# An opening in smaller loads, and breaks in the matmul order of the first three blocks (hybrid encoder layer, one core)

## The chip, the cores and the metric

The kernel runs on one core of a Trainium2 chip. Its time is the device time of one execution in microseconds; of several runs the median is given. Matrix products run on TensorE (PE in the profile, PEld for its weight loads), elementwise work on VectorE (DVE), ScalarE (ACT) and GpSimd (POOL). Transfers are issued by SyncE (SP) and by ScalarE.

## The reference

One encoder layer on 256 tokens of 2048 channels, in float32:

```python
hn = _rmsnorm(h, norm_w[i])
proj = hn @ w_in[i]                       # 2048 x 18432, nine groups of 2048 columns
q, v, f_fwd, f_bwd, z_a, b_gate, c_gate, h_b, z_b = jnp.split(proj, IN_SPLITS, axis=-1)
o_a = _hgrn2_bidirectional(jax.nn.silu(q), v, f_fwd, f_bwd, lb_all[:, i])
o_a = _head_rmsnorm(o_a, hgrn_norm_w[i]) * jax.nn.silu(z_a)
y_b = b_gate * _short_conv(c_gate * h_b, conv_w[i])
o_b = _rmsnorm(y_b, conv_norm_w[i]) * jax.nn.silu(z_b)
h = h + jnp.concatenate([o_a, o_b], axis=-1) @ w_out[i]
h = h + (p[i] @ w_ple[i]) * jax.nn.sigmoid(h @ w_ple_gate[i])
return _rmsnorm(h, final_norm_w)
```

The weights are large (211 MB are read) and the products with them are nearly all of the work.

## The kernel before

**Products in split form.** Every float32 operand is split into a high part, rounded to the matmul's format (fp32r), and the rest, a low part. ScalarE casts the high part (line 74), VectorE subtracts it (line 75). A product is then high times both parts plus low times high. In the blocks of this change (lines 299 to 312) a block is 256 output columns, over 16 k-tiles of 128 rows. For each k-tile and each half of 128 columns (m = 0, 1) there are two matmuls: a *long* one, the high part of the weights with both parts of x (512 columns, line 309), and a *short* one, the low part of the weights with the high part of x (256 columns, line 307). Four matmuls, each with its own weight load, make a tile of a block. Their order is `PLAIN`: long, short, long, short. A table can give single tiles another order: `OUTER` is long, short, short, long, and `SHORTS` is short, short, long, long. `ONE` and `BOTH` put such a break into tile 1, or into tiles 1 and 5, of some later blocks.

**Opening.** x comes transposed, scaled by the norm weights (`x_split`, lines 249 and 250: the high part on ScalarE, the low part on VectorE); the row norms come later, as a factor. The vectors (norm weights and nine others, 80 KB) are one load on ScalarE's queue (line 155). SP loads x and the weights: first k-tiles 0 and 1 of x, then of the first block's weights, then k-tiles 2 and 3 of both, then the rest in pieces of four k-tiles. Loads use eight semaphores in turn, so that a load waits on its queue until the load eight before it has landed. Meanwhile 13 matmuls of zeros run on TensorE (line 179).

**The first three blocks** (forward and backward forget gates and q of the first head pair) are worked through side by side: four groups g of four k-tiles, and in each the three blocks c = 0, 1, 2. This part is written in order by hand for ScalarE, VectorE and TensorE. With c = 0 comes the split of x. I call a pair (g, c) a part.

**Behind it** a planner orders the instructions of each engine by priorities and its own costs; TensorE works through block after block, and the recurrent mixing of the pair of heads (scans, exponentials, products on GpSimd, then small score matmuls, lines 506 and 550) is put in between at fixed numbers of tiles. The four matmuls `rps` (line 284), which spread the row norms, come behind the 14th tile of the fourth block.

Of the kernel before, what the change touches and what calls it, by code (L numbers as in the profile page):

```python
# [88 lines left out]
def tile_hymba_encoder(  # L89
# [14 lines left out]
    nc = tc.nc  # L104
# [16 lines left out]
    ws = Stream(tc, rawp, splp, 3)  # L121
# [29 lines left out]
    def load_x(k0, k1):  # L151
        nc.sync.dma_start(xf32[:, k0:k1], xt[:, k0:k1])

    vec = const.tile([P, 10, 16], F32, name="vec")
    nc.scalar.dma_start(vec, vecs)

    for k0 in (0, 2):
        load_x(k0, k0 + 2)
        ws.load(0, k0, k0 + 2)
    for g in range(4):  # L160
        if g:
            load_x(4 * g, 4 * g + 4)
# [12 lines left out]

    act.activation(dummy[:, 0:1], wz[:, 0:1], AF.Copy)
    wps = psm.tile([P, 512], F32, tag="y", name="wps")
    for _ in range(13):
        pe.matmul(wps[:, :P], lhsT=wz, rhs=wz, start=True, stop=True)

    epst = const.tile([P, 1], F32, name="epst")
# [35 lines left out]
    def lower_bounds():  # L217
        dve.tensor_tensor(out=mx, in0=th[:, :, 0, :], in1=th[:, :, 1, :], op=ALU.max)
        for j in range(2):
            dve.tensor_tensor(out=et[:, :, j, :], in0=th[:, :, j, :], in1=mx, op=ALU.subtract)  # L220
        act.activation(et, et, AF.Exp)
        dve.tensor_tensor(out=esum, in0=et[:, :, 0, :], in1=et[:, :, 1, :], op=ALU.add)
        dve.reciprocal(out=esum, in_=esum)
        dve.tensor_tensor(out=lb, in0=et[:, :, 0, :], in1=esum, op=ALU.mult)
        dve.tensor_scalar(lb, lb, 2.0**-63, None, op0=ALU.max)
        dve.tensor_tensor(out=oml, in0=et[:, :, 1, :], in1=esum, op=ALU.mult)
        dve.tensor_scalar(noml, oml, -1.0, None, op0=ALU.mult)
# [8 lines left out]
    def tick():  # L236
        now[0] += 1
        due = sorted(e for e in pend if e[0] <= now[0])
        for e in due:
            pend.remove(e)  # L240
        for e in due:
            e[2]()
# [5 lines left out]
    def x_split(kt):  # L248
        act.activation(xs[:, kt, 0, :], xf32[:, kt, :], AF.Copy, scale=nw[:, kt : kt + 1])
        dve.scalar_tensor_tensor(  # L250
            out=xs[:, kt, 1, :], in0=xf32[:, kt, :], scalar=nw[:, kt : kt + 1],
            in1=xs[:, kt, 0, :], op0=ALU.mult, op1=ALU.subtract,
        )
# [35 lines left out]
    def acc_in(c, i):  # L289
        return [psg.tile([P, 2, T], F32, tag="g", name=f"a{c}_{i}_{m}") for m in range(2)]  # L290
# [3 lines left out]
    OUTER = ((0, 0), (0, 1), (1, 1), (1, 0))  # L294
    SHORTS = ((0, 1), (1, 1), (0, 0), (1, 0))
# [3 lines left out]
    def gemm_part(acc, w, g, k0=0, k1=4, orders={}):  # L299

        for k in range(k0, k1):
            kt = 4 * g + k
            for m, short in orders.get(kt, PLAIN):
                a = acc[m].rearrange("p a b -> p (a b)")
                lhsT = w[:, k, short, m * P : (m + 1) * P]
                if short:
                    pe.matmul(a[:, :T], lhsT=lhsT, rhs=xs[:, kt, 0, :], start=False, stop=(kt == NKT - 1))  # L307
                else:
                    pe.matmul(  # L309
                        a, lhsT=lhsT, rhs=xs[:, kt, :, :].rearrange("p s n -> p (s n)"), start=(kt == 0), stop=False  # L310
                    )
            tick()
# [37 lines left out]
    ids3 = [blocks[c, 0] for c in first]  # L350
    acc3 = [acc_in(c, 0) for c in first[:2]]
    acc3.append([psm.tile([P, 2, T], F32, tag=t, name=f"a{B_Q}_0_{m}") for m, t in enumerate(("x", "y"))])
    with tc.manual_schedule(engines={ENG.Activation, ENG.DVE, ENG.PE}):
        for g in range(4):
            for c in range(3):
                half, v = ws.open(ids3[c][g])

                n = 2 if g or c else 1
                for k0 in range(0, 4, n):
                    if c == 0:  # L360
                        for k in range(k0, k0 + n):
                            x_split(4 * g + k)
                    ws.split(half[:, k0 : k0 + n], v[:, k0 : k0 + n])
                    gemm_part(acc3[c], v, g, k0, k0 + n)
            if g == 2:
                lower_bounds()
    rctx.close()
# [544 lines left out]
```

## Time and profile before

| | us |
|---|---|
| three timed runs | 1127.13, 1127.22, 1128.06 |
| median | 1127.22 |
| profiled execution | 1127.79 |
| its span in the trace | 1126.1 |
| TensorE busy in the span | 1116.5 |
| mean granted clock of TensorE | 0.998 |

The span begins with the first instruction and ends with the last; 1.69 us of the profiled execution lie outside it. A row of the timeline gives start and duration in microseconds, engine, line, operation, output and inputs; merged rows give their count, and in brackets stands how long the engine had been idle and for whom it waited. A matmul's duration includes its way through the array, so that successive matmuls overlap in the records; the pace is read from starts.

### The profile page before, as it was taken

What the parts mean: (1) busy time and instruction counts of PE and PEld (TensorE: products, weight loads), DVE (VectorE), ACT (ScalarE), POOL (GpSimd) and SP (SyncE); (2) the same over time, 40 slices, a digit from 0 to 9 for tenths busy, and PEclk for the clock granted to TensorE, in tenths of its full rate; (3) what the DMA queues carried; (4) which work ended last, traced back from release to release, by engine and by line L of the source; (5) the groups of instructions that cost most, each with busy time, mean ns of one, the idle gap of its engine ahead of it and who ended that gap; (6) DMA issues with size and microseconds to landing.
All of it is one profiled execution on the core that took longest, in us unless ns stands there. A gap on an engine that the chain in (4) does not pass through costs nothing.

```text
span 1126.1 us, 16341 instructions
## 1 busy us (share of the span) xinstructions
PE 1116.5 (99%) x6530; PEld 959.9 (85%) x6530; DVE 728.5 (65%) x920; ACT 629.4 (56%) x868; POOL 217.8 (19%) x167
## 2 busy tenths in 40 slices
PE   9999999999999999999999999999999999999996
PEld 8888888888888888888888888888888888888886
DVE  7798476956876587766655665565565555545664
ACT  7696577756775586564454454444445434444553
POOL 1144025300622034221121111121220000000112
PEclk9999999999999999999999999999999999999999
DMA  9746445555545455555555565555557555556542
GB/s 352 268 168 209 155 160 188 159 188 181 201 135 209 163 169 169 192 182 187 188 191 187 182 200 196 194 192 192 188 188 270 187 186 187 187 203 212 201 169 75
DMA packets 37371, 214.25 MB, mean 190 GB/s; under 512 B 4144, under 2 KB 4528, under 8 KB 17584
## 3 DMA queue, kind: packets, MB, share of 16 engines
q1 hardware_dynamic: 37008, 212.88, 54.4%
q8 instruction: 51, 0.84, 0.3%
q10 hardware_dynamic: 288, 0.34, 0.1%
q14 instruction: 24, 0.20, 0.1%
HBM read 211.11 MB, written 2.10 MB: 189 GB/s over the span
## 4 chain that ended last, share of the span: by engine, by line
PE 99%; ACT 0%; DVE 0%; DVEq 0%; issue 0%; ACTq 0%
PE a L309 37%; PE a L307 18%; PE a L330 5%; PE a L328 5%; PE a L329 5%; PE pg L736 3%; PE pg L735 3%; PE pg L737 3%; PE pa L735 3%; PE pa L736 3%; PE pa L737 3%; PE pb L736 3%; PE pb L735 3%; PE pb L737 3%; PE scps L506 1%; PE cx L550 1%
## 5 line engine op out<-in xcount | busy, mean ns | idle before, releaser
L75 DVE TENSOR_TENSOR spl<-raw,spl 128x1024 fp32r<-128x1024 f32 (+2 forms) x398 | 498.5, 1259 | 309.3 <-ACT spl L74 309.1
L309 PE MATMUL a<-xs,spl 128*128 128x512 f32 x1792 | 620.6, 394 | 0.0
L74 ACT CAST spl<-raw 128x1024 fp32r<-128x1024 f32 (+2 forms) x398 | 403.2, 1019 | 329.2 <-PE a L307 164.7
L307 PE MATMUL a<-xs,spl 128*128 128x256 f32 x1792 | 493.2, 278 | 0.0
L309 PEld LDWEIGHTS a<-xs,spl 128*128 128x128 f32 x1792 | 335.0, 188 | 76.9
L307 PEld LDWEIGHTS a<-xs,spl 128*128 128x128 f32 x1792 | 335.9, 188 | 1.9 <-DVE spl L75 0.2
L328 PE MATMUL a<-spl,xs 128*128 128x512 f32 x256 | 100.8, 394 | 0.0
L330 PE MATMUL a<-spl,xs 128*128 128x512 f32 x256 | 99.8, 390 | 0.0
L329 PE MATMUL a<-spl,xs 128*128 128x512 f32 x256 | 99.6, 389 | 0.0
L341 ACT COPY r<-a 128x256 f32<-128x256 f32 x112 | 40.9, 368 | 56.0 <-PE a L307 56.0
L795 POOL TENSOR_TENSOR hh<-hh,fw 128x512 f32<-128x512 f32 (+1 forms) x9 | 11.7, 1311 | 260.4 <-ACT gt L794 257.8
L330 PEld LDWEIGHTS a<-spl,xs 128*128 128x128 f32 x256 | 48.1, 188 | 10.1
L328 PEld LDWEIGHTS a<-spl,xs 128*128 128x128 f32 x256 | 48.1, 188 | 9.6
L329 PEld LDWEIGHTS a<-spl,xs 128*128 128x128 f32 x256 | 48.1, 188 | 9.5
L735 PE MATMUL pa<-spl,mixa 128*128 128x512 f32 x128 | 50.1, 392 | 0.0
L737 PE MATMUL pa<-spl,mixa 128*128 128x512 f32 x128 | 49.8, 389 | 0.0
L736 PE MATMUL pa<-spl,mixa 128*128 128x512 f32 x128 | 49.8, 389 | 0.0
L735 PE MATMUL pb<-spl,mixb 128*128 128x512 f32 x128 | 49.8, 389 | 0.0
L736 PE MATMUL pb<-spl,mixb 128*128 128x512 f32 x128 | 49.8, 389 | 0.0
L737 PE MATMUL pb<-spl,mixb 128*128 128x512 f32 x128 | 49.8, 389 | 0.0
L346 POOL TENSOR_TENSOR xf<-xf,rbc 128x1024 f32<-128x1024 f32 x8 | 19.8, 2477 | 131.1 <-DVE xf L342 124.0
L735 PE MATMUL pg<-spl,ht 128*128 128x512 f32 (+1 forms) x120 | 45.1, 376 | 0.0
(183 smaller groups left out, 1170.6 us busy)
## 6 DMA issues: line engine op xcount, KB each, us to landing
raw<-in_w_in_dram SPq DMA_DIRECT2D x106, 1024.0 KB, 4.9
raw<-in_w_in_dram SPq DMA_DIRECT2D x74, 512.0 KB, 4.9
raw<-in_w_out_dram SPq DMA_DIRECT2D x32, 1024.0 KB, 4.8
raw<-in_w_gate_dram SPq DMA_DIRECT2D x12, 1024.0 KB, 4.8
raw<-in_w_gate_end_dram SPq DMA_DIRECT2D x8, 512.0 KB, 4.8
xf<-in_xtok_dram SPq DMA_DIRECT2D x2, 1024.0 KB, 11.9
hh<-in_xtok_dram SPq DMA_DIRECT2D x1, 2048.0 KB, 8.0
raw<-in_w_ple_dram SPq DMA_DIRECT2D x4, 512.0 KB, 3.4
```

The source lines that it names most:

```text
L74: self.nc.scalar.copy(out=v[:, :, 0], in_=r)
L75: self.nc.vector.tensor_tensor(out=v[:, :, 1], in0=r, in1=v[:, :, 0], op=ALU.subtract)
L307: pe.matmul(a[:, :T], lhsT=lhsT, rhs=xs[:, kt, 0, :], start=False, stop=(kt == NKT - 1))
L309: pe.matmul(a, lhsT=lhsT, rhs=xs[:, kt, :, :].rearrange("p s n -> p (s n)"), start=(kt == 0), stop=False)
L328: pe.matmul(acc[m], lhsT=lh, rhs=w[:, kt % 2, 0, :], start=(kt == 0), stop=False)
L329: pe.matmul(acc[m], lhsT=lh, rhs=w[:, kt % 2, 1, :], start=False, stop=False)
L330: pe.matmul(acc[m], lhsT=ll, rhs=w[:, kt % 2, 0, :], start=False, stop=(kt == NKT - 1))
L341: act.copy(out=r, in_=acc[m][:, 1, :])
L346: pool.tensor_tensor(out=t, in0=t, in1=r.unsqueeze(1).broadcast_to([P, n, T]), op=ALU.mult)
L735: pe.matmul(acc[m], lhsT=lh, rhs=wh, start=(kt == 0), stop=False)
L736: pe.matmul(acc[m], lhsT=lh, rhs=wl, start=False, stop=False)
L737: pe.matmul(acc[m], lhsT=ll, rhs=wh, start=False, stop=(kt == nk - 1))
```

## The change

Four edits. The norm weights are loaded on their own (8 KB, 64 bytes a partition) ahead of the nine other vectors, both from ScalarE. The first two k-tiles of x and of the first block's weights come in pieces of one k-tile (128 KB each). The zero calls are 11 in place of 13. In six of the twelve parts of the first three blocks, from (0, 1) to (2, 0), the part's second tile gets a break, `OUTER` and `SHORTS` in turn.

```diff
     vec = const.tile([P, 10, 16], F32, name="vec")
-    nc.scalar.dma_start(vec, vecs)
-
-    for k0 in (0, 2):
-        load_x(k0, k0 + 2)
-        ws.load(0, k0, k0 + 2)
+    nc.scalar.dma_start(vec[:, 0], vecs[:, 0])
+    nc.scalar.dma_start(vec[:, 1:], vecs[:, 1:])
+
+    for k0, k1 in ((0, 1), (1, 2), (2, 4)):
+        load_x(k0, k1)
+        ws.load(0, k0, k1)
...
-    for _ in range(13):
+    for _ in range(11):
         pe.matmul(wps[:, :P], lhsT=wz, rhs=wz, start=True, stop=True)
...
+    turns = ((0, 1), (0, 2), (1, 0), (1, 1), (1, 2), (2, 0))
+    kicks = {(g, c): {4 * g + 1: (OUTER, SHORTS)[n % 2]} for n, (g, c) in enumerate(turns)}
...
-                    gemm_part(acc3[c], v, g, k0, k0 + n)
+                    gemm_part(acc3[c], v, g, k0, k0 + n, kicks.get((g, c), {}))
```

What it moves, from the order of instructions of both kernels. In the changed kernel's rows the line numbers are one higher up to the first three blocks, and four higher behind them. First TensorE in part (0, 1), tiles 0 and 1 (`a_0_0` and `a_0_1` are the block's two halves, `spl` the split weights). Before:

```order
L309 MATMUL a_0_0_167<-xs,spl_206 128x512
L307 MATMUL a_0_0_167<-xs,spl_206 128x256
L309 MATMUL a_0_1_168<-xs,spl_206 128x512
L307 MATMUL a_0_1_168<-xs,spl_206 128x256
L309 MATMUL a_0_0_167<-xs,spl_206 128x512
L307 MATMUL a_0_0_167<-xs,spl_206 128x256
L309 MATMUL a_0_1_168<-xs,spl_206 128x512
L307 MATMUL a_0_1_168<-xs,spl_206 128x256
```

and the same tiles of part (0, 2) in the changed kernel:

```order
L310 MATMUL a_0_0_170<-xs,spl_228 128x512
L308 MATMUL a_0_0_170<-xs,spl_228 128x256
L310 MATMUL a_0_1_171<-xs,spl_228 128x512
L308 MATMUL a_0_1_171<-xs,spl_228 128x256
L308 MATMUL a_0_0_170<-xs,spl_228 128x256
L308 MATMUL a_0_1_171<-xs,spl_228 128x256
L310 MATMUL a_0_0_170<-xs,spl_228 128x512
L310 MATMUL a_0_1_171<-xs,spl_228 128x512
```

The second tile has both shorts ahead of both longs; in part (0, 1) its order is long, short, short, long. Elsewhere TensorE's order is the same in both kernels but for the two zero calls.

SP at the start (`xf` is x, `raw` the weights as loaded; `DMAHW0` to `DMAHW7` are the eight semaphores, of which vec takes the first). Before:

```order
L152 DMA xf_80<-in_xt_dram 128x512
L58 DMA raw_84<-in_w_in_dram 128x512
L152 DMA xf_80<-in_xt_dram 128x512
L58 DMA raw_84<-in_w_in_dram 128x512
L58 DMA raw_88<-in_w_in_dram 128x512 x2
L58 DMA raw_91<-in_w_in_dram 128x1024
L152 DMA xf_80<-in_xt_dram 128x1024 [waits DMAHW0_49]
L58 DMA raw_84<-in_w_in_dram 128x1024 [waits DMAHW1_49]
```

Now:

```order
L152 DMA xf_80<-in_xt_dram 128x256
L58 DMA raw_85<-in_w_in_dram 128x256
L152 DMA xf_80<-in_xt_dram 128x256
L58 DMA raw_85<-in_w_in_dram 128x256
L152 DMA xf_80<-in_xt_dram 128x512
L58 DMA raw_85<-in_w_in_dram 128x512
L58 DMA raw_91<-in_w_in_dram 128x512 [waits DMAHW0_49]
L58 DMA raw_91<-in_w_in_dram 128x512 [waits DMAHW1_49]
L58 DMA raw_94<-in_w_in_dram 128x1024 [waits DMAHW2_49]
L152 DMA xf_80<-in_xt_dram 128x1024 [waits DMAHW3_49]
```

The waits begin with the second block's first half (`raw_91`); the third block's first load (`raw_94`) now waits for the second vec load.

ScalarE while the second head pair's forget gates are prepared (`lf` their logarithms, `dd` and `pf` the exponentials of the first pair, `sq` the gate of q). Before:

```order
L477 ACTIVATE dd_640<-dd_640 128x512
L399 ACT_TABLE_LOAD
L399 ACTIVATE lf_864<-xf_503,lb,oml 128x256 x2
L74 CAST spl_908<-raw_890 128x2x512
L399 ACTIVATE lf_864<-xf_503,lb,oml 128x256
L392 ACT_TABLE_LOAD
L392 ACTIVATE sq_861<-qt_504 128x512
```

Now:

```order
L480 ACTIVATE pf_640<-dd_641 128x512
L403 ACT_TABLE_LOAD
L403 ACTIVATE lf_865<-xf_504,lb,oml 128x256
L481 ACT_TABLE_LOAD
L481 ACTIVATE dd_641<-dd_641 128x512
L74 CAST spl_909<-raw_891 128x2x512
L403 ACT_TABLE_LOAD
L403 ACTIVATE lf_865<-xf_504,lb,oml 128x256 x2
L396 ACT_TABLE_LOAD
L396 ACTIVATE sq_862<-qt_505 128x512
```

One exponential of `pf` and the last of `dd` come later, between the logarithms, with two more table loads. VectorE's order changes in the same stretch in the same manner; GpSimd's order does not change.

## The prediction

> **What bounds the kernel now.** I read the page first (busy shares, then the chain of waits), then the opening 15 us row by row, then the pace of TensorE in stretches of equal work, and last the place near 110 us where the order on ScalarE changes.
>
> ```profile
> span 1126.1 us, 16341 instructions
> PE 1116.5 (99%) x6530; PEld 959.9 (85%) x6530; DVE 728.5 (65%) x920; ACT 629.4 (56%) x868; POOL 217.8 (19%) x167
> PE 99%; ACT 0%; DVE 0%; DVEq 0%; issue 0%; ACTq 0%
> ```
>
> TensorE is busy for 99% of the span and is 99% of the chain that ends last. The kernel can become faster only where TensorE starts its real work earlier, or where the same matmuls follow each other more closely. Both are small. The opening, from the timeline of the three engines:
>
> ```profile
> 1.12 5.37 PE L179 MATMUL wps<-wz 128*128 128x128 f32 x26 [1.12 <-DVE wz L174]
> 5.20 0.51 ACT L249 ACTIVATE xs<-xf,vec 128x256 fp32r<-128x256 f32 x1 [2.46 <-DMA vec<-in_vecs_dram]
> 5.81 0.41 ACT L74 CAST spl<-raw 128x256 fp32r<-128x256 f32 x1
> 6.37 0.47 PE L309 MATMUL a<-xs,spl 128*128 128x512 f32 x1
> 7.25 0.41 ACT L74 CAST spl<-raw 128x256 fp32r<-128x256 f32 x1
> 8.53 1.75 DVE L75 TENSOR_TENSOR spl<-raw,spl 128x256 fp32r<-128x256 f32 x3
> 9.08 0.31 PE L307 MATMUL a<-xs,spl 128*128 128x256 f32 x1
> 9.57 0.39 PE L309 MATMUL a<-xs,spl 128*128 128x512 f32 x1
> 11.40 1.29 DVE L75 TENSOR_TENSOR spl<-raw,spl 128x512 fp32r<-128x512 f32 x2 [1.13 <-ACT spl L74]
> 12.39 0.40 PE L309 MATMUL a<-xs,spl 128*128 128x512 f32 x1
> ```
>
> Zero matmuls fill TensorE from 1.12 us. ScalarE waits 2.46 us for the norm weights (5.20), casts the first weight tile (5.81), and the first real matmul starts at 6.37. The first four k-tiles are then paced by ScalarE and VectorE: the split of the fourth is the first of the three that start at 8.53, and its short matmul starts at 9.08, right behind it. The next part starts at 9.57.
>
> **Pace.** A k-tile is four matmuls: two long (512 columns, line 309) and two short (256 columns, line 307). I cut windows at the start of a tile, so that two hold the same 16 tiles, and a third holds the 57 tiles after the first four:
>
> ```profile
> 18.05:29.35 11.30, 11.30 (x34) 6.01 (x33) 1.00 1.03 415
> 148.74:159.83 11.09, 11.09 (x33) 6.00 (x33) 1.00 0.55 191
> 9.57:49.85 40.28, 40.28 (x115) 21.43 (x115) 1.00 0.85 339
> 50.55 0.60 PE L284 MATMUL rps<-ident,rw 128*128 128x128 f32 x4
> ```
>
> (The rows are those of line 309; the first number is the width, and the counts include matmuls that hang over an edge.) The same 16 tiles take 11.30 us early and 11.09 us later, at the same granted clock (1.00): 0.7067 us a tile (40.28/57 gives the same) against 0.6931 us, 13.6 ns less. TensorE waits for nothing in either window, so this is a state of the matmul stream, and it holds for 40 us: it ends where the four small matmuls of the norms (50.55) interrupt the stream.
>
> **The change part by part.**
>
> *Norm weights alone, smaller first pieces, fewer zero calls.* Three things must be there for the first real matmul: norm weights, a piece of x, a piece of weights.
>
> ```profile
> vec<-in_vecs_dram ACTq DMA_DIRECT2D x1, 80.0 KB, 4.4
> xf<-in_xt_dram SPq DMA_DIRECT2D x2, 256.0 KB, 4.4
> raw<-in_w_in_dram SPq DMA_DIRECT2D x4, 256.0 KB, 5.1
> q1 hardware_dynamic: 873, 1.65, 69.5%
> q10 hardware_dynamic: 144, 0.08, 5.6%
> 0.80 0.39 SPq L152 DMA_DIRECT2D xf<-in_xt_dram  x1
> 2.18 1.92 SPq L58 DMA_DIRECT2D raw<-in_w_in_dram  x4
> 5.19 0.33 SPq L152 DMA_DIRECT2D xf<-in_xt_dram  x1
> 2.00:4.00 2.00, 2.00 (x11) 2.00 (x11) 0.19 (x1) 0.73 (x2) 2.00 (x8) 1.00 0.91 223
> L179 PE MATMUL wps<-wz x26: 275/421/582, 1.1 to 6.2; 128*128 128x128 f32 x26
> ```
>
> Ahead of the first cast stood 80 + 256 + 256 = 592 KB (there at 5.81 at the latest); now 80 + 128 + 128 = 336 KB, what before had come by 5.20 (vec and the first x). So the first cast moves from 5.81 to about 5.2, and TensorE's first real matmul is ready near 5.2 + (6.37 - 5.81) = 5.8. The zero calls: 26 passes in 5.37 us, 22 of them end near 1.12 + 5.37 x 22/26 = 5.7. Removing two calls is thus needed for the earlier start, and by itself worth nothing. The start gains about 0.5 us.
>
> That gain does not last, I think. The third k-tile needs the second half of the first weight block. In the kernel before, ScalarE cast it at 7.25. After the change the same 80 + 1024 KB must still land ahead of that cast, in more packets. If it lands when it did, casts and splits of the third and fourth tiles run as before: fourth split from 8.53, next part at 9.57, and the gain is nil, since every short matmul there starts right behind its split. More packets: the 144 of vec took 5.6% of 16 engines over 8 us, 7.2 engine-us or 50 ns each; 144 more on 16 engines are at most 0.45 us, and at least nothing, since the bytes are equal. I take 0.1 us lost at 9.57, bounds 0.45 lost to 0.54 gained: the upper one because the third weight block's first half was split at 11.40 + 0.65 = 12.05, with its first matmul at 12.39 and its first short one a third of a tile, 0.24, later, so no earlier start can be worth more than some 0.34 + 0.24 = 0.58 less a semaphore, say 0.54, from there on unless that load comes earlier too.
>
> The issue order on SP hides one more thing. Eight loads are in flight on eight semaphores; the ninth waits for the first to land (5.19, when vec was there). Two vec loads and smaller pieces use them up sooner: the third block's 512 KB is now issued when the second vec load lands (about 5.2; before, it was the last of the four issued by 4.10). The cover is what is queued ahead of it: 80 + 4 x 128 + 4 x 256 KB, of which some 0.7 MB are there by 5.2 (at 223 GB/s, the stretch 2 to 4 us, from 2.0 on), so 0.9 MB are left, 2.2 us at 415 GB/s (the windows above). An issue reaches the engines in less: the first one starts at 0.80 and they are 0.91 busy from 2.00. Nothing is lost; without that cover the 1.2 us between issue and transfer would be.
>
> The Trainium skill, DMA: Bandwidth & Descriptors, section Issuing engines are not separate DMA queues, says that transfers issued from different engines share the same 16 engines and interleave. The trace agrees (80 KB on ScalarE's queue took 4.4 us, as 256 KB on SP's), and by it the rest of vec still gets in the way of the pieces behind it, which speaks for the lost 0.1 rather than the gain.
>
> *Breaks.* Six of the twelve parts of the first three blocks get one tile in another order: long-short-short-long (OUTER) in three, both shorts before both longs (SHORTS) in three. The number of matmuls and columns is the same. The kernel before has such breaks later; two of them, with the tile ahead and the tile behind:
>
> ```profile
> 52.38 0.39 PE L309 MATMUL a<-xs,spl 128*128 128x512 f32 x1
> 54.48 0.39 PE L309 MATMUL a<-xs,spl 128*128 128x512 f32 x1
> 126.51 0.39 PE L309 MATMUL a<-xs,spl 128*128 128x512 f32 x1
> 128.60 0.40 PE L309 MATMUL a<-xs,spl 128*128 128x512 f32 x1
> ```
>
> Three tiles with a SHORTS break take 2.10 and 2.09 us against 3 x 0.693 = 2.08: a break costs up to 0.02 us and leaves the quick pace quick. Whether one turns the slow pace into the quick one no row shows directly: at 126.51 it comes one tile after another kind of matmul, too soon to tell the pace ahead of it. What speaks for it: the pace changed at a single interruption (50.55) and never by itself in 57 tiles. I take it that the first SHORTS break does it. It sits in the tenth tile; the tiles behind it to the interruption are 61 - 10 = 51, worth 51 x 13.6 ns = 0.69 us, less 6 x 0.02 = 0.12 for the breaks: 0.57 us. Bounds: 0.12 lost to 0.76 gained (all 57 tiles quick at once, breaks free, is 0.78). No new wait: a broken tile is the second of a piece whose split the first has used already.
>
> *What the planner does with it.* Behind the first blocks the order on TensorE is unchanged, but on ScalarE two table loads are added between 78 and 90 us, and one exponential is moved behind an evacuation.
>
> ```profile
> 74.65 1.15 ACT L476 ACTIVATE pf<-dd 128x512 f32<-128x512 f32 x2
> 78.34 1.28 ACT L399 ACT_TABLE_LOAD   x1
> 86.88 1.98 ACT L74 CAST spl<-raw 128x1024 fp32r<-128x1024 f32 x2
> 87.95 2.36 DVE L75 TENSOR_TENSOR spl<-raw,spl 128x1024 fp32r<-128x1024 f32 x2 [0.21 <-ACT spl L74]
> 90.23 1.38 DVE L554 COPY_PREDICATED scm<-tri,scps 128x512 f32<-128x512 uint32 x2
> 105.51 0.62 POOL L487 TENSOR_TENSOR kc<-dd,ge 128x256 f32<-128x256 f32 x1
> 106.21 1.91 POOL L493 TENSOR_TENSOR kx<-kc,ge 128x512 f32<-128x512 f32 x1
> 110.25 1.27 PE scps L506 x63
> 111.52 1.09 PE cx L550 x8
> ```
>
> Two loads of 1.28 and one half of 1.15 are 3.1 us on ScalarE ahead of the two casts at 86.88. VectorE works in order: their subtractions (87.95) and the masked copies (90.23) move by as much, and behind those stand the scans from which GpSimd makes kc and kx for the second pair. kx ends at 108.12, so at 111.2; TensorE wants it at 111.52, less the 0.47 it is early by then, 111.05. The scores at 110.25 need only kc (106.13, then 109.2, against 109.8). So kx comes about 0.2 us late: I take 0.2 lost, bounds 0 and 1.3 (one table load more than I count, 1.28).
>
> **Sum.** -0.57 (pace) + 0.1 (start) + 0.2 (kx) = -0.27 us. The profiled execution took 1127.79 us, its span and 1.69 around it: it becomes 1127.5. The three timed runs have a median of 1127.22, 0.57 below the profiled one, so the timed median becomes 1126.95; I say **1126.9 us**.
>
> **Rivals.**
> 1. *Breaks change nothing in the pace.* For it: the same four matmuls, and no row shows a slow stretch cured by one. Against it: the end of the slow pace at an interruption. Then +0.12 + 0.1 + 0.2 = +0.4 on the median of 1127.22: 1127.6. The Trainium skill, TensorE: Matmul & The Clock Gate, section Back-to-back issue gap, lets the distance of matmuls follow from their columns, which makes it this rival. The trace does not bear that rule out: equal columns took 11.30 and 11.09 us.
> 2. *The start is kept.* The second half of the first block lands earlier than at 7.25, and 0.5 us stays: -0.57 - 0.5 + 0.2 = -0.9, 1126.3. For it: ScalarE and VectorE have done the first two tiles sooner. Against it: equal bytes, DMA saturated.
> 3. *Slower: kx is late in earnest.* One place (the cx matmuls after the second scores), one chain (table loads, casts, masked copies, scans, kx). It decides from the point where kx ends later than 111.05. With 1.3 us lost there the sum is -0.57 + 0.1 + 1.3 = +0.8: 1127.22 + 0.8 = 1128.0. For it: VectorE and GpSimd had no gaps to absorb 3.1 us between 87.95 and 108.12 but ScalarE's own; against it: the slack of 3.4 us covers nearly all.
>
> **How the numbers follow.** Forecast 0.52, rival 1 0.20, rival 2 0.12, rival 3 0.13, something larger 0.03 (a slow pace that a break starts and that stays for hundreds of tiles at 13.6 ns). The range reaches from rival 2 with some luck in the landings to rival 3: 1126.1 to 1128.0. What a measurement of this kernel can tell from no change is about 0.2%, 2.25 us. None of the cases reaches it, so: within 0.95, faster 0.02, slower 0.03.
>
> **What would show it.** The first real matmul starts near 5.8, yet the second part starts at 9.5 to 9.7 (right), or at 9.1 (rival 2). Windows of 16 tiles between 15 and 49 us are 11.1 wide (right) or 11.3 (rival 1). TensorE shows a wait at the second cx matmuls of about 0.2 (right), none, or 1 us (rival 3). From 130 us on every stretch lies earlier by one constant amount; if that amount changes later, or is above 1.2 us either way, my account of what bounds the kernel is wrong.

## The result, and the profile after

| | before | after |
|---|---|---|
| median of the runs of this comparison, us | 1127.85 (10 runs, 1127.12 to 1128.10) | 1130.34 (10 runs, 1129.85 to 1131.50) |
| ratio, 95% interval | | 1.0025 (1.0015 to 1.0035) |
| profiled execution, us | 1127.79 | 1130.32 |
| its span, us | 1126.1 | 1128.3 |
| outside the span, us | 1.69 | 2.02 |

The changed kernel is slower by 2.49 us (0.22% by the two medians, 0.25% by the ratio). The forecast was 1126.9 with 1128.0 as the upper end. The page of the changed kernel still shows TensorE busy for 99% of the span, but its chain of waits is no longer all TensorE:

```profile
span 1128.3 us, 16338 instructions
PE 1116.1 (99%) x6526; PEld 959.4 (85%) x6526; DVE 725.4 (64%) x920; ACT 632.0 (56%) x870; POOL 217.2 (19%) x167
PE 93%; DVE 2%; ACT 2%; POOL 1%; issue 1%; DMA 0%; SPq 0%; DVEq 0%; ACTq 0%
```

The first row of its list of TensorE's waits lies in the opening, the third at the second pair's cx matmuls; the second is the wait of the zero calls for their zeros, which the kernel before has too:

```profile
PE a L310 <- ACT spl L74: 1.4, 1, 1.4
PE wps L180 <- DVE wz L175: 1.1, 1, 1.1
PE cx L554 <- POOL kx L497: 1.1, 1, 1.1
```

**The opening**, from the timeline of the changed kernel (SP's issues, ScalarE's casts, TensorE's long matmuls):

```profile
2.65 0.43 SPq L152 DMA_DIRECT2D xf<-in_xt_dram  x1
3.13 1.86 SPq L58 DMA_DIRECT2D raw<-in_w_in_dram  x4
5.83 0.54 PE L310 MATMUL a<-xs,spl 128*128 128x512 f32 x1
8.48 0.40 ACT L74 CAST spl<-raw 128x256 fp32r<-128x256 f32 x1 [1.56 <-DMA raw<-in_w_in_dram]
8.94 0.50 PE L310 MATMUL a<-xs,spl 128*128 128x512 f32 x1 [1.39 <-ACT spl L74]
10.78 0.39 PE L310 MATMUL a<-xs,spl 128*128 128x512 f32 x1
```

Real work starts at 5.83 (before 6.37), as forecast. But the third k-tile's weights are cast at 8.48 rather than at 7.25, ScalarE having waited 1.56 us for them, and part (0, 1) starts at 10.78 rather than 9.57.

**The pace.** Windows of 16 tiles in the changed kernel (rows of line 310: tiles 17 to 32 and 33 to 48, then the fifth block):

```profile
19.15:30.28 11.13, 10.68 (x33) 5.78 (x33) 1.00 1.03 414
30.28:41.37 11.09, 11.09 (x33) 6.00 (x33) 1.00 0.96 399
52.92:64.19 11.27, 11.08 (x33) 5.93 (x33) 1.00 0.72 248
```

The first holds three breaks and takes 11.13, the second none and takes 11.09: the quick pace. The third window is the fifth block, which in the profile of the kernel before was quick (63.49 - 52.38 = 11.11 us) and now takes 11.27.

**The second head pair.** The chain of waits of the changed kernel, in order of time (start, length):

```profile
91.39 0.95 ACT spl L74
...
94.72 1.29 DVE scm L558 x2
...
103.50 3.34 POOL kc L491
106.84 3.12 POOL qc L491 x2
109.96 1.57 POOL kc L491
111.53 0.07 issue
111.60 1.92 POOL kx L497
113.52 0.04 issue
113.56 0.49 PE cx L554 x2
```

kx starts at 111.60 where it started at 106.21, and TensorE waits for it. Behind that nothing changes any more. The accounts of the two profiled executions differ by 2.53 us, and where the difference arises is read from the starts of the same tiles:

| from the start to | before | after | offset | added here |
|---|---|---|---|---|
| part (0, 1) | 9.57 | 10.78 | +1.21 | +1.21, start |
| fifth block | 52.38 | 52.92 | +0.54 | -0.67, pace |
| sixth block | 63.49 | 64.19 | +0.70 | +0.16, fifth block slow |
| seventh block of this kind | 126.51 | 128.63 | +2.12 | +1.42, kx (1.39) and the first tiles of the sixth block |
| end of the span | 1126.1 | 1128.3 | +2.2 | +0.1 |
| device time | 1127.79 | 1130.32 | +2.53 | +0.33, outside the span |

### The profile page after: what moved, and what is told of

Read it like the earlier page. It is cut to its first block, busy times and chain, and to the rows that moved or that the text cites. A ratio compares the mean times of both kernels' runs of the same rounds, so it can differ in the third digit from the quotient of the medians.

```text
span 1128.3 us, 16338 instructions
## 1 busy us (share of the span) xinstructions
PE 1116.1 (99%) x6526; PEld 959.4 (85%) x6526; DVE 725.4 (64%) x920; ACT 632.0 (56%) x870; POOL 217.2 (19%) x167
## 4 chain that ended last, share of the span: by engine, by line
PE 93%; DVE 2%; ACT 2%; POOL 1%; issue 1%; DMA 0%; SPq 0%; DVEq 0%; ACTq 0%
PE a L310 35%; PE a L308 18%; PE a L329 4%; PE a L331 4%; PE a L330 4%; PE pg L740 3%; PE pg L739 3%; PE pg L741 3%; PE pa L739 3%; PE pa L741 3%; PE pa L740 3%; PE pb L741 3%; PE pb L740 3%; PE pb L739 3%; PE cx L554 1%; PE scps L510 1%
```

## Experiments

Each kernel is the kernel before with the edit named, unless it says otherwise. "Part (0, 1)" is the start of the fifth tile on TensorE; the kernel before has it at 9.57 in the profile of the prediction.

### One part of the change at a time

**Breaks alone** (the `turns` and `kicks` lines of the change and nothing else).

> The kernel before with the six breaks alone; loads, 13 zero calls and the order of ScalarE and VectorE stay as before. My account of the changed kernel (start +1.2 us, pace -0.67, wait for kx +1.35): only the pace term is left. Part (0,1) begins at 9.57 as before, the tiles behind the first break take 0.693 us instead of 0.707, the third block ends 0.6 to 0.7 us earlier, no wait at the second cx matmuls; total -0.4 to -0.7, the less the more tiles the fourth and fifth block run at the slow pace. Rival (the quick pace came from the later, interrupted start and not from the breaks): tiles stay at 0.707, total 0 to +0.1.

Measured 1127.43 against 1127.86 for the kernel before beside it, ratio 0.9998 (0.9989 to 1.0007). Part (0, 1) starts at 9.62, no wait for kx. Two windows of 16 tiles, the last of the first three blocks and the fifth block:

```profile
29.20:40.30 11.10, 11.10 (x33) 6.01 (x33) 1.00 0.98 406
51.85:63.12 11.27, 11.08 (x33) 5.93 (x33) 1.00 0.68 241
```

The pace is quick in the first blocks and slow in the fifth, as in the whole change. The gain is not to be told from no change.

**Eleven zero calls alone.**

```diff
-    for _ in range(13):
+    for _ in range(11):
```

> The kernel before with 11 zero calls in place of 13, nothing else. On ScalarE and VectorE this alone gives the order of the changed kernel, with the two added table loads. My account: the start does not move (first real matmul at 6.37, part (0,1) at 9.57, pace slow), and TensorE waits at the second cx matmuls for kx: 1.0 to 1.9 us, total +1.0 to +1.9. Rival (the wait at cx comes from the late start of the blocks, not from the order): no wait there, total 0.

Measured 1129.37, ratio 1.0014 (1.0005 to 1.0024). Part (0, 1) starts at 9.39, so the start is no later, and the pace is slow throughout. The window of tiles 17 to 32:

```profile
18.24:29.55 11.31, 11.31 (x33) 6.02 (x33) 1.00 1.03 417
```

But TensorE waits for kx, as its timeline shows:

```profile
113.23 1.16 PE L550 MATMUL cx<-qc,kx 128*128 128x128 f32 x8 [1.06 <-POOL kx L493]
```

Two zero matmuls less in the first six microseconds cost 1.4 us at 113 (from the sixth block of this kind to the seventh it takes 128.29 - 63.90 = 64.39 us, in the kernel before 126.51 - 63.49 = 63.02): with 11 of them the order of ScalarE's and VectorE's instructions is that of the whole change, with the two added table loads, which the breaks and the split of vec do not bring (their orders, apart from the edit itself, are those of the kernel before). The 128 KB pieces alone bring it too.

**The change with 15 zero calls**, for which the planner returns to ScalarE's and VectorE's order of before.

```diff
-    for _ in range(11):
+    for _ in range(15):
```

> The changed kernel with 15 zero calls in place of 11. With that number ScalarE and VectorE get the order of the kernel before. My account: the opening is as in the changed kernel (part (0,1) near 10.8, since TensorE waits for loads there anyway), the quick pace stays, and the wait at the second cx matmuls is gone: 1.2 to 1.5 us faster than the changed kernel, within 0 to +0.8 of the kernel before. Rival (late start sets the wait): as slow as the changed kernel, +2.2 to +2.5.

Measured 1128.88, ratio 1.0010 (1.0001 to 1.0019): 1.46 us less than the whole change. That is 1.02 above the kernel before beside it, more than the 0.8 that was allowed. Part (0, 1) starts at 10.71, as late as with 11 calls, the pace is quick, and TensorE does not wait at its second cx matmuls:

```profile
112.48 1.16 PE L554 MATMUL cx<-qc,kx 128*128 128x128 f32 x8
```

So the wait for kx follows the order and not the late start: it is there with a start that is not late (eleven zero calls) and gone with a late one. All five kernels with that order have the wait, 1.06 us each; no other kernel here has it.

**128 KB pieces alone** (`load_x` and `ws.load` for (0, 1), (1, 2), (2, 4)).

> The kernel before with the first two k-tiles in pieces of 128 KB, vec in one load, 13 zero calls, no breaks. ScalarE and VectorE get the order of the changed kernel. If the small pieces slow the loads: the weights of k-tiles 2 and 3 land near 8.4 instead of 7.2, part (0,1) begins at 10.4 or later. If the split of vec does: part (0,1) at 9.6 to 9.8. In both cases the slow pace in the first three blocks and a wait at the second cx matmuls of 0.5 to 1.5 us; total +1.7 to +2.8 in the first case, +0.7 to +1.7 in the second.

Measured 1130.73, ratio 1.0028 (1.0017 to 1.0039): the whole loss from this edit alone. Its profiled execution, 1129.68, is the lowest of its eight; part (0, 1) starts at 10.16 there, TensorE waits for kx, and 2.08 us lie outside the span. And the pace is quick, without a single break in the first three blocks:

```profile
18.90:30.00 11.10, 11.10 (x33) 6.01 (x33) 1.00 1.03 413
```

**Norm weights on their own** (the two `vec` loads).

> The kernel before with the norm weights loaded on their own ahead of the other vectors, nothing else; ScalarE and VectorE keep the order of the kernel before. If the small load of 64 bytes a partition is part of the late start: part (0,1) begins at 9.9 to 10.2, total +0.3 to +0.6. If the pieces of 128 KB are all of it: part (0,1) at 9.4 to 9.7, total -0.2 to +0.2.

Measured 1127.69 against 1127.74, ratio 1.0000 (0.9991 to 1.0009); 1.73 us outside the span. It costs nothing and brings nothing.

### Why the pieces make the start late

**Pieces with x on ScalarE's queue**, 15 zero calls, no breaks, vec as before.

```diff
     for k0, k1 in ((0, 1), (1, 2), (2, 4)):
-        load_x(k0, k1)
+        nc.scalar.dma_start(xf32[:, k0:k1], xt[:, k0:k1])
         ws.load(0, k0, k1)
```

> Pieces of 128 KB as in the changed kernel, but those of x issued from ScalarE's queue and those of the weights from SP's, vec in one load, 15 zero calls, no breaks; ScalarE's order has no added table loads. If SP's issue rate (one piece in 0.47 us) limits the loads: the first block's second half is there near 7.3, part (0,1) begins at 9.7 or earlier, total -0.3 to +0.6. If it is the packets (1 KB in place of 2 KB) that slow the engines: part (0,1) at 10.2 to 10.8, total +0.6 to +1.7.

**Pieces on SP as in the change**, 15 zero calls, no breaks, vec as before: ScalarE's and VectorE's order of before, so no wait for kx; the start by itself.

> Pieces of 128 KB alone with 15 zero calls, by which ScalarE and VectorE get the order of the kernel before. My account: as with the pieces alone but without the wait at the second cx matmuls: 1.2 to 1.5 us less than with the pieces alone, +1.2 to +1.7 against the kernel before, of which 0.35 lie outside the span. Rival (the late loads are what makes cx wait): +2.5 to +2.9.

Measured 1130.09 with two queues, ratio 1.0020 (1.0011 to 1.0029), and 1129.28 with one, ratio 1.0015 (1.0006 to 1.0025). Part (0, 1) starts at 11.41 and 11.17. With two queues the rate of the loads from 4 to 8 us is that of the kernel before again (last column, GB/s):

```profile
4.00:6.00 2.00, 2.00 (x12) 2.00 (x11) 0.17 (x1) 0.90 (x3) 0.12 (x2) 1.00 0.90 303
6.00:8.00 2.00, 1.77 (x14) 1.44 (x12) 1.39 (x4) 0.90 (x3) 0.00 (x0) 1.00 1.00 305
```

but it does not help: the timeline of ScalarE has it wait at 8.70 for the third k-tile's x, which it had issued itself by 2.66. The expectation of neither theory came: part (0, 1) starts later than 9.7 and later than 10.8, and the time is 2.35 above the kernel before beside it, where 1.7 was the most expected.

```profile
8.70 0.51 ACT L249 ACTIVATE xs<-xf,vec 128x256 fp32r<-128x256 f32 x1 [1.18 <-DMA xf<-in_xt_dram]
```

In the whole change the same windows show less:

```profile
4.00:6.00 2.00, 2.00 (x12) 2.00 (x11) 1.36 (x3) 1.14 (x3) 0.12 (x2) 1.00 0.74 224
6.00:8.00 2.00, 1.55 (x9) 1.09 (x8) 0.91 (x2) 0.69 (x2) 0.00 (x0) 1.00 0.99 268
```

and in the kernel before 327 and 300:

```profile
4.00:6.00 2.00, 2.00 (x13) 2.00 (x12) 0.26 (x1) 0.69 (x2) 0.10 (x2) 1.00 0.97 327
6.00:8.00 2.00, 2.00 (x13) 1.50 (x12) 1.98 (x6) 2.00 (x7) 0.00 (x0) 1.00 1.02 300
```

**Pieces cut across the partitions**, so that each row of a transfer stays 2 KB (13 zero calls, no breaks).

```diff
-    for k0 in (0, 2):
-        load_x(k0, k0 + 2)
-        ws.load(0, k0, k0 + 2)
+    for k0 in (0, 2):
+        for p in ((0, 64), (64, 128)) if k0 == 0 else ((0, 128),):
+            load_x(k0, k0 + 2, *p)
+        for p in ((0, 64), (64, 128)) if k0 == 0 else ((0, 128),):
+            ws.load(0, k0, k0 + 2, p=p)
```

> The first two k-tiles as two 128 KB pieces each again, but cut across the partitions (0 to 63, 64 to 127) rather than across the k-tiles, so that a row of a transfer stays 2 KB; no split of vec, 13 zero calls, no new breaks. If it is the 1 KB rows that slow the loads down: 300 GB/s or more from 4 us on as in the kernel before, the third weight piece's conversion by 7.5, part (0,1) by 9.6, and 1.7 us outside the span. If it is the number of transfers (the time to issue each, and what each costs before it moves): about 230 GB/s from 4 to 6 us, part (0,1) at 10.1 or later, and 2.05 us outside the span. The second cx waits about 1.2 for kx either way, since the order behind the third block is that of the change.

The window of 4 to 6 us, and two rows of the timeline (SP and ScalarE):

```profile
4.00:6.00 2.00, 2.00 (x12) 2.00 (x11) 0.48 (x1) 0.51 (x1) 0.10 (x2) 1.00 0.68 203
```

```profile
3.95 1.85 SPq L58 DMA_DIRECT2D raw<-in_w_in_dram  x4
9.26 0.40 ACT L74 CAST spl<-raw 128x256 fp32r<-128x256 f32 x1 [1.47 <-DMA raw<-in_w_in_dram]
```

One execution, 1131.55. Part (0, 1) starts at 11.56 and the loads move 203 GB/s from 4 to 6 us, so a late start does not need 1 KB rows; that they play no part where they occur is not shown. TensorE waits 1.06 for kx here too, as expected.

With all these loads on SP's queue, the later SP issues the third k-tile's weights, the later they are cast: issued at 2.18, 3.13 and 3.95 (kernel before, change, this one), cast at 7.25, 8.48 and 9.26. In the change two more pieces stand ahead of them, 0.47 each, so the issue is 0.95 later where the cast is 1.23 later. But the time of the issue does not decide it alone. Issued at 3.12 to 3.16, these weights landed anywhere from 7.8 to 8.9 in four profiles (the change, the change with 15 zero calls, and the pieces with 13 and with 15). And with two queues SP issues them earlier than the kernel before does:

```profile
1.71 0.42 SPq L58 DMA_DIRECT2D raw<-in_w_in_dram  x1
```

There it is the third k-tile's x that is late: issued at 2.21, it lands 6.5 us later, where in the kernel before it was issued at 1.72 and took 4.7. SP, which has fewer loads to issue there, sends off the second block's first load at 2.18, and the two land together, at 8.5 and 8.7. So that kernel speaks against the issue time as the whole cause, but as it also moves another load forward it does not rule it out as a part. How much of the 1.23 is the later issue stays open.

The Trainium skill, DMA: Bandwidth & Descriptors, section Issuing engines are not separate DMA queues, says that issuing from several engines saves only the time to start a transfer, which it calls usually small. That the second queue made the start no earlier agrees with it (11.41 against 11.17). One start took SP 0.47 us here, against 5.0 us from issue to landing of the third k-tile's weights in the kernel before.

The time outside the span is 1.75 with pieces cut across the partitions, not 2.05: that expectation of the theory of the number of transfers failed.

### Whether breaks change the pace

**Breaks less one later break.** The kernel with breaks, and without the `ONE` break that the kernel before already has in the fifth block.

```diff
-            kick = {(0, 1): ({}, ONE, BOTH)}.get(...)
+            kick = {(0, 1): ({}, {}, BOTH)}.get(...)
```

> The kernel with the six breaks alone, and without the single SHORTS break of the fifth block (B_FB of the second head). In the traces so far a SHORTS break that follows tiles with durations 392 and 395 ns of their two long matmuls turns the quick pace into the slow one, and in the kernel with breaks alone that happens in the fifth block. My account: without it all tiles up to the sixth block are quick, 0.2 to 0.25 us less than with breaks alone, total -0.5 to -0.8 against the kernel before. Rival (breaks do not set the pace): as with breaks alone, -0.4, and blocks five and six slow.

Measured 1127.46 against 1127.74, ratio 0.9998 (0.9989 to 1.0007). The fifth block, with the quick pace ahead of it, keeps it: 16 tiles in 11.10 where breaks alone took 11.27.

```profile
28.96:40.05 11.09, 11.09 (x33) 6.00 (x33) 1.00 1.00 413
51.60:62.70 11.10, 11.10 (x34) 6.01 (x33) 1.00 0.67 232
```

So a SHORTS break can turn the quick pace into the slow one. Its median is not below that of breaks alone (1127.46 and 1127.43), where 0.2 to 0.25 less was expected, and neither is to be told from the kernel before.

**Eleven zero calls with breaks**: the kernel of the second experiment, which was slow throughout, plus the breaks.

> The 11 zero calls and the new breaks, without the split of vec and the 128 KB pieces: the run with 11 zero calls alone (1129.37 us), plus the breaks and nothing else. That run kept the slow pace (0.707 us a tile) from its first tile to the fifth block, so this is the clean test of whether breaks turn slow into quick. If they do (the prediction's theory): quick from one of the three SHORTS tiles on (tiles 10, 18 or 26), which saves 38 to 54 tiles x 0.0135 = 0.5 to 0.7 us by the fifth block's start, where part of it goes back (the fifth block's own ONE break turns quick to slow, 0.2): about 1128.9, and the second cx still waits about 1.2 for kx. If they don't (rival: only an idle stretch of TensorE in the opening sets the pace): 0.707 throughout the first three blocks and 1129.4.

Measured 1128.71, ratio 1.0010 (1.0000 to 1.0019). Part (0, 1) starts at 9.57; the starts of tiles 7 to 10 are 0.694, 0.711 and 0.700 apart, the last two as in the slow cycle; the tenth tile is the first SHORTS break, and from the next on the pace is quick. The last 16 tiles of the first three blocks, and the fifth block:

```profile
29.10:40.19 11.09, 11.09 (x33) 6.00 (x33) 1.00 0.98 404
51.74:63.01 11.27, 11.08 (x33) 5.93 (x33) 1.00 0.72 254
```

The wait for kx, from the timeline, is there as without breaks:

```profile
112.37 1.16 PE L553 MATMUL cx<-qc,kx 128*128 128x128 f32 x8 [1.06 <-POOL kx L496]
```

From part (0, 1) to the fifth block it takes 51.74 - 9.57 = 42.17 us; without breaks it took 52.61 - 9.39 = 43.22, of which 0.35 are two stalls in tiles 7 and 9 of that profile. The rest, 0.7, is the pace. The medians, 1128.71 and 1129.37, point the same way, but against the kernel before beside each the two differ less (1.36 and 1.51) than the intervals are wide.

**A late start with breaks**: 20 zero calls, so that TensorE finds its data there, and the breaks.

> The kernel before with the new breaks and 20 zero calls, so that TensorE starts late (first real matmul at about 8.5) with all its data there and has no idle stretch in the opening. Theory that breaks act only by the state they meet: the tiles ahead of the first break have either pace; an OUTER tile leaves slow slow and quick quick, a SHORTS tile turns slow to quick in one of the phases of the slow cycle and not in the others, and leaves quick quick; so the pace is 0.693 from tile 10, 18 or 26 on. Rival (breaks do nothing, the opening's wait does all): the pace that stands at tile 4 stands to the end of the third block.

One execution, 1127.86. TensorE's long matmuls at the starts of tiles 2, 5, 6, 8 and 9 (the sixth tile, at 10.75, is the first break, OUTER):

```profile
7.92 0.40 PE L309 MATMUL a<-xs,spl 128*128 128x512 f32 x1
10.04 0.40 PE L309 MATMUL a<-xs,spl 128*128 128x512 f32 x1
10.75 0.40 PE L309 MATMUL a<-xs,spl 128*128 128x512 f32 x1
12.16 0.39 PE L309 MATMUL a<-xs,spl 128*128 128x512 f32 x1
12.85 0.39 PE L309 MATMUL a<-xs,spl 128*128 128x512 f32 x1
```

Four tiles from 7.92 to 10.75 take 2.83, 0.707 each; behind the break a tile takes 0.69 (12.16 to 12.85), and it stays so. No stall and no other operation lies between. Here an OUTER break made slow quick, ahead of the first SHORTS break in the tenth tile, which the theory had left to SHORTS alone.

Over all profiles: the last 16 tiles of the first three blocks are quick in all six kernels with the breaks, and in five of the eleven profiles without them.

**The kernel before, four more profiles.**

> The kernel before, unchanged, for one more profile. Its run times lie in two groups, about 1127.0 and 1127.9. If the groups are the two paces, this profile's span and its pace agree: about 1125.3 with 0.693 us a tile in the first three blocks, or about 1126.2 with 0.707. If the groups come from elsewhere (the memory, the end), a span of 1125.3 can have the slow pace.

> The kernel before, unchanged, one of three more profiles. If its short spans (about 1125.3) come from the pace, such a profile has 11.10 us for 16 tiles in the first three blocks; if they come from the opening's loads, it has 11.30 us and part (0, 1) starts earlier than 9.57. A span near 1126.1 or above has 11.30 by both.

(The other two ask the same question.) What they show, with the profile of the prediction as the first row:

| span, us | part (0, 1) | stalls in the tiles behind it | tiles 17 to 32, us |
|---|---|---|---|
| 1126.1 | 9.57 | none | 11.30 |
| 1127.1 | 9.87 | tiles 6, 7 | 11.30 |
| 1125.7 | 9.40 | tile 7 | 11.10 |
| 1126.7 | 9.26 | tiles 7, 9 | 11.31 |
| 1125.2 | 9.27 | tile 9 | 11.10 |

The kernel before thus has either pace by chance, quick in two of five. A stall in the opening can leave the quick pace behind it (the last row: slow up to tile 8, quick from tile 10) or the slow one (the fourth). The spread of its spans is the pace (0.7 to 0.8) and the stalls themselves (tile 7 of the second row takes 1.30 rather than 0.71). Halves by partition, with its late start, had the slow pace too (11.31 for these tiles): a wait in the opening does not always leave the quick one. The fifth block, with its `ONE` break, is quick in four of the five and slow (11.30) in the fourth.

## Why the prediction was wrong, step by step

From the forecast, 1126.95 ahead of rounding, to 1130.34 it is 3.39 us: 0.63 because ten runs put the median of the kernel before at 1127.85 rather than 1127.22, 0.27 forecast as a gain, and 2.49 lost.

**The zero calls and the first matmul: the time was right, in part by luck.** It forecast 5.8 and 5.83 came. Of the two terms behind it, the end of the zero matmuls was right (near 5.7; the last one starts at 5.76 and the first real matmul follows it). The loads were not: the first cast was put at 5.2 and came at 4.03, and as TensorE was still at its zeros, the error did not show.

```profile
4.03 0.41 ACT L74 CAST spl<-raw 128x256 fp32r<-128x256 f32 x1
```

That two calls less are "by itself worth nothing" was wrong as a sentence on the whole kernel: through the planner they cost a wait at 113 us (1129.37 with that edit alone).

**The start: the term was mis-sized, and this is one of the two steps that failed.** "I take 0.1 us lost at 9.57, bounds 0.45 lost to 0.54 gained"; measured were 1.21 lost in the profiles. The step rested on "if it lands when it did", and the price of more transfers was taken from their packets alone. The row that shows a price of the pieces other than their packets was quoted there: SP's issues at 0.80 and 2.18 are 0.46 apart each, so two more pieces ahead of the third k-tile's weights issue it 0.95 later (2.18 to 3.13), and its cast came 1.23 later. The text looked at the issue of the ninth load, and did not ask what becomes of the sixth. The upper bound of the loss, too, was set by packets, not by issues. Shown: the pieces alone make the start late (10.16 to 11.41 in five profiles with k-tile pieces, 9.06 to 9.87 in the ten without any pieces at 11 or 13 zero calls), and with 2 KB rows the start is late as well (11.56). Open: how much of the delay is the later issue, and what makes up the rest.

**kx: the mechanism was right and its size was not, the second failed step.** "I take 0.2 lost, bounds 0 and 1.3"; measured were 1.39: the cx matmuls start 2.11 later (113.56 for 111.45), the output matmuls ahead of the scores only 0.72 (109.03 for 108.31). Of it 1.06 stands in the profile as a wait. It is rival 3, at its price. Two terms were missing. First, the casts came 4.41 later (91.29 for 86.88), not 3.1: ScalarE reached the table load ahead of them 1.05 later (79.39 for 78.34), most of it because the whole program was late by 0.70 there, and partly since its order differs further ahead. Second, GpSimd's step from kc to kx was taken as fixed. The chain after shows the second kc at 1.57 us where it had been 0.62. In the timeline of the changed kernel VectorE works beside it without a gap:

```profile
105.14 7.46 DVE L75 TENSOR_TENSOR spl<-raw,spl 128x1024 fp32r<-128x1024 f32 x5
109.93 1.59 POOL L491 TENSOR_TENSOR kc<-dd,ge 128x256 f32<-128x256 f32 x1
111.60 1.91 POOL L497 TENSOR_TENSOR kx<-kc,ge 128x512 f32<-128x512 f32 x1
```

In the kernel before, the subtraction beside that kc had to wait for its cast:

```profile
105.52 1.70 DVE L75 TENSOR_TENSOR spl<-raw,spl 128x1024 fp32r<-128x1024 f32 x1 [0.44 <-ACT spl L74]
```

The two ran side by side there too, but kc began first, at 105.51, took 0.62, and the subtraction took 1.70 where the next one, by itself, takes 1.23. In the changed kernel the fourth of the five subtractions had begun at 109.41, and kc took 1.59. So it is the one that begins second that is slow. The kernel with the norm weights on their own shows it without the changed order:

```profile
105.71 1.22 DVE L75 TENSOR_TENSOR spl<-raw,spl 128x1024 fp32r<-128x1024 f32 x1 [0.42 <-ACT spl L74]
105.73 1.68 POOL L488 TENSOR_TENSOR kc<-dd,ge 128x256 f32<-128x256 f32 x1
```

There the subtraction began 0.02 us ahead and kc took 1.68, but kx behind it, with VectorE idle for most of that time, only 1.05. In the changed kernel the next subtraction follows without a gap, and both kc and kx are slow. So kx is 4.41 + 0.97 = 5.4 later, and the slack of 3.4 with the 0.72 that TensorE itself is late does not cover that. That the order is the cause is shown (eleven zero calls have the wait with an early start, the change with 15 has none with a late one); that GpSimd's operation waits for a VectorE subtraction that began ahead of it is read from these rows and was not tested by itself. The Trainium skill, GPSIMD Engine Reference, section Key points, states that GpSimd shares its SBUF interfaces with VectorE and contends with VectorE's instructions that have two SBUF inputs, as these subtractions do; the rows agree with it: kc takes 0.62 us where it begins first, and 1.59 and 1.68 where a subtraction is under way.

**The pace: right in size, wrong in two of its parts.** 0.57 was forecast, 0.67 measured between the two profiles. That breaks can turn the slow pace quick, which no row had shown, is shown by the kernels with eleven and with 20 zero calls; rival 1 falls. But in the profiled execution of the change the state was quick before the tenth tile, and the pieces alone gave it without breaks: there the stall of the opening can have done it, or the OUTER break in the sixth tile; the record does not tell which. "Leaves the quick pace quick" was wrong: the one break in the fifth block turned quick into slow and cost 0.16 in that block; the sixth block's second break, a SHORTS one, made it quick again. It had been read from two breaks, at 52.38 and 126.51. And the gain was counted from a profile with the slow pace as though every execution had it; two of five profiles of the kernel before are quick already, so that on the median the breaks are worth less, 0.43 by the medians of breaks alone, within what can't be told from nothing.

**What lies outside the span** was taken to stay at 1.69. It is 2.05 to 2.11 in the medians of all five kernels with k-tile pieces, and 1.72 to 1.74 in those of the others with several runs. It goes with these pieces, but not with the number of transfers (1.75 with halves by partition). What it is stays open.

**Rival 2** (the start is kept) fell with the cast at 8.48. The forecast's last test, an offset that stays constant from 130 us on, held: +2.12 at 128.63, +2.2 at the end. That it should not be above 1.2 failed by size: what bounds the kernel is as described, but the two small places cost more than they were given.

## What to carry to other kernels

Cutting the first loads smaller moves the later loads on that queue back by one issue time for each added piece (0.47 us here), and here they landed later by more than that: list issue and landing of each load that the opening waits for, not only of the first ones. A gain of tenths on the engine that bounds the kernel is easily outweighed by what a planner does with the edit elsewhere, even with an edit as far off as two zero matmuls; where the instruction order changes, follow the changed chain to its end with the durations it will have beside its new neighbours. And a profile is one execution: before a state in it is priced as a gain, look in more of them at how often it occurs.

## What was not expected of the hardware

The same four matmuls of a tile follow each other in 0.693 us or in 0.707 us, for dozens of tiles, at the same granted clock (1.00) and without any wait. The state is kept until something breaks the rhythm. By the starts the slow state is a cycle of three tiles (710, 711, 699 ns). What a break does depends on the tile that it meets, and this shows in how long the trace records that tile's two long matmuls. The SHORTS break of the fifth block stands in 16 of the 17 profiles. Behind a tile with 391 and 391 ns the pace stays quick (four profiles, that of the kernel before in the prediction among them); behind one with 392 and 395 ns, a quick tile as well, it turns slow (six, the change among them); behind a slow tile with 398 and 395 ns it turns quick (four), and behind one with 395 and 403 ns it stays slow (two). None of the 16 departs from this: the 0.16 us that this break cost in the change goes with the tile ahead of it. The SHORTS break that made slow quick in eleven zero calls with breaks stands behind 398 and 395 ns too. An OUTER break made it quick behind 403 and 398 ns (20 zero calls) and left it slow behind 395 and 403 ns (breaks less one). What the state is, the records do not show.
